# Moving the first parts of stationary weight blocks to the placement of their second parts

## The chip, the cores and the metric

The kernel runs on one core of one Trainium2 chip. The metric is device time in microseconds (us) of the whole kernel, which is one launch. An engine is named as in the profile: PE is the matrix engine, PEld its weight loads, DVE the vector engine, ACT the scalar engine, POOL the GpSimd engine, SP the engine that issues most DMAs.

## The reference, cut to what matters

The program is a two-layer decoder trunk on 256 positions of width 2048: a Mamba-2 layer and then a sparse-attention layer, each with a wide input projection, a gate and an output projection. Everything is fp32. The weights, some 230 MB, are read from HBM once. The change is about the two wide projections that are computed transposed, channels by positions:

```python
def ssd_mixer(x, w_in, conv_w, ...):
    proj = x @ w_in                      # 256 x 2048 by 2048 x 10304
    z, xbc, dt = jnp.split(proj, ...)
    ...
def dsa_mixer(x, w_in, ...):
    proj = x @ w_in
    c_q, c_kv, k_idx, w_idx, gate = jnp.split(proj, [s1, s2, s3, s4], -1)
    ...
    return (o * jax.nn.silu(gate)) @ w_out
```

## The kernel before, in words

**Products in parts.** PE multiplies in a format that is narrower than fp32 (`F32R`). To keep the precision, each fp32 operand is split into a first part `h` (its rounding to that format) and a second part `l` (what the rounding left). A product is then three matmuls: first by first, first by second, second by first. `Stream` does this for weights. A unit is one block of 128 x 1024 weights: SP loads it into one of four `raw` buffers (line 93), ACT rounds it into `h` (line 109), DVE subtracts to get `l` (line 138), and PE uses both. Four units are split ahead of the one that PE is on (`SPLIT`), so a unit's conversions are due some four units before its matmuls.

**The stage that the change touches.** `stream_w` (from line 306) computes 128 channels by 256 positions out of two units. The first unit of a pair (`half == 0`, use `FIRST8`) holds row tiles 0 to 7 of the 2048 input rows, the second (`half == 1`, use `OTHERS`) row tiles 8 to 15. A row tile is 128 x 128 weights, which PE holds stationary, while 256 columns of the input stream past them ("moving"). The input is stored as `xT` (in the second layer `x1T`): for each row tile 256 first parts, and right behind them 256 second parts. So each `h` tile is loaded twice in a row, once for each part of the input (line 328), and each `l` tile once (line 324). Each unit has 16 matmuls with `h` and 8 with `l`. In a `FIRST8` unit the `h` matmuls come first, in the order 0 to 7, and the `l` matmuls follow in the order 0, 1, 6, 7, 4, 5, 2, 3. In an `OTHERS` unit the `l` matmuls come first. There are 80 pairs of units in the first layer (accumulator `acc` in the trace) and 32 pairs in the second (`g`, the gate), which makes 112 pairs and 3584 matmuls with `h`. Between units the kernel puts the small matmuls of the scan and of the heads.

All other units have use `MOVING` or are read by other code: there the weights are cut in the same way, and none of their matmuls is touched.

**Where the parts lie.** `places` (line 123) gives each unit its two places in SBUF. The first part has a plain block of 1024 numbers (4096 bytes in each partition). The second part has a buffer of 1088 numbers (4352 bytes), and lies in it in one of three ways: for `FIRST8` as four chunks of 256 numbers that begin 272 numbers (1088 bytes) apart, for `OTHERS` as one block that begins 16 numbers (64 bytes) into the buffer, else as one block from its start. In the built program `xT` (byte 20,992), `x1T` (86,528) and all buffers of `h` (135,680 on, 4096 apart) and `l` (152,064 on, 4352 apart) begin at multiples of 256 bytes. A moving slice is 1024 bytes long and also begins at such a multiple; a row tile's weights are 512 bytes. What is called **offset** below is the start of the stationary weights less the start of the moving slice, in bytes, modulo 256:

| matmuls | offset before, by row tile |
|---|---|
| `h`, both kinds of unit | 0 for all |
| `l` of `FIRST8` | 0 for tiles 0 and 1, 64 for 2 and 3, 128 for 4 and 5, 192 for 6 and 7 |
| `l` of `OTHERS` | 64 for all |

**What sets the order.** The kernel is written under a manual schedule: each engine runs its instructions in the order in which the program issues them, and waits on semaphores where it reads what another engine writes. `Stream.run` issues a unit's conversions, its matmuls, and then one step of every piece of side work that is active. For a head of the attention layer one such step writes `og` (line 978, DVE), a later one rounds it (line 985, ACT), and the next subtracts (line 987, DVE); `og` has three buffers.

Of the kernel before, what the change touches and what calls it, by code (L numbers as in the profile page):

```python
# [9 lines left out]
F32 = mybir.dt.float32  # L10
F32R = mybir.dt.float32r
I32 = mybir.dt.int32
AF = mybir.ActivationFunctionType
# [3 lines left out]
P = 128  # L17
T = 256
# [41 lines left out]
MOVING, FIRST8, OTHERS = range(3)  # L60
# [9 lines left out]
class Stream:  # L70
# [22 lines left out]
            self.nc.sync.dma_start(r[:, :u.width], u.src)  # L93
            self.raws[i] = r

    def pieces(self, i):

        w = self.units[i].width
        n = w // 2 if i == 0 else w
        return [slice(a, a + n) for a in range(0, w, n)]  # L100

    def convert(self, i, eng, later=False):

        if i < len(self.units):
            w = self.units[i].width
            r = self.raws.pop(i)
            h, l = self.places(i)
            for cs in self.pieces(i):
                self.nc.scalar.activation(h[:, cs], r[:, cs], AF.Copy)  # L109
            self.parts[i] = (h, l)  # L110
            a, b = r[:, :w], h[:, :w].bitcast(F32)
            if len(l.shape) == 3:
                a, b = (t.rearrange("p (a b) -> p a b", a=4) for t in (a, b))
            else:
                l = l[:, :w]
            self.halfway[i] = (l, a, b)
        if not later:
            self.finish(i, eng)

    def places(self, i):  # L120

        if i in self.homes:
            pool, o = self.homes[i]
            return [pool.tile([P, 1088], F32R, tag=t, name=f"{t}{i}")[:, o:o + 1024]
                    for t in ("hi", "lo")]
        h = self.whi.tile([P, 1024], F32R, tag="hi", name=f"hi{i}")
        t = self.wlo.tile([P, 1088], F32R, tag="lo", name=f"lo{i}")  # L130
        use = self.units[i].use
        if use == FIRST8:
            return h, t.rearrange("p (a b) -> p a b", a=4)[:, :, 0:256]
        return h, t[:, 16:1040] if use == OTHERS else t[:, 0:1024]

    def finish(self, i, eng):
        if i in self.halfway:
# [33 lines left out]
def trunk_kernel(ctx: ExitStack, tc: tile.TileContext, x, xt, w1, wdt, dtp, prm, wo1,  # L171
                 wkv, wcq, wix, wg, wab, wo2, lnr, out):
    nc = tc.nc
# [15 lines left out]
    def acc_tile(name):  # L189
        return p_acc.tile([P, 512], F32, tag="acc", name=name)  # L190

    def y_tile(name):
        return p_y.tile([P, 512], F32, tag="y", name=name)
# [116 lines left out]
    def stream_w(half, cell, name, turn=True):  # L310


        def pe(h, l):
            if half == 0:
                cell["ps"] = acc_tile(name)[:, 0:T]
            ps, xs = cell["ps"], cell["x"][0]
            first, second = (1, 0) if half and turn else (0, 1)
            for lo in (first, second):
                for k in (0, 1, 6, 7, 4, 5, 2, 3) if lo and half == 0 else range(8):
                    kt, w = half * 8 + k, slice(k * P, (k + 1) * P)  # L320
                    last = half == 1 and lo == second and k == 7
                    if lo:
                        lw = l[:, w] if half else l[:, k // 2, k % 2 * P:(k % 2 + 1) * P]
                        nc.tensor.matmul(ps, lw, xs[:, kt, 0:T], start=False,  # L324
                                         stop=last, skip_group_check=True)
                    else:
                        for c in range(2):
                            nc.tensor.matmul(ps, h[:, w], xs[:, kt, c * T:(c + 1) * T],  # L328
                                             start=(kt == 0 and c == 0), stop=last and c == 1,
                                             skip_group_check=True)  # L330
        return pe
# [183 lines left out]
    for g in range(NG):  # L515
        for kind, n in (("B", 1), ("C", 1), ("x", 4), ("z", 4)):
            for ci in range(n):
                cell = {"x": xcell}
                for half in range(2):
                    k = len(st.units)  # L520
                    i = st.add(w1[k], 1024, stream_w(half, cell, f"acc{k}", turn=k > 1),
                               OTHERS if half else FIRST8)
# [72 lines left out]
    for g in range(NG):  # L595
        u = 20 * g
# [75 lines left out]
    for n in range(2):  # L672
        cs = slice(n * 1024, (n + 1) * 1024)
# [120 lines left out]
    for kb in range(8):  # L794
        i = st.add(wcq[kb], 1024, stream_tok(kb, 512, cells["q"], "qp",
                                             held if kb < EARLY else None), MOVING)
    st.side(i, (lat_norm, cells["q"], 512, PC_QG, 4, "q", "cqT"))
    for kb in range(8):
        i = st.add(wkv[kb], 672, stream_tok(kb, 336, cells["kv"], "kvp"), MOVING)
# [7 lines left out]
    def idx_pe(q, cell):  # L807
        def pe(h, l):
            cell["ps"] = acc_tile(f"ix{q}")
            for k in range(2):  # L810
                ps = cell["ps"][:, k * T:(k + 1) * T]
                for kt in range(4):
                    o = (k * 4 + kt) * P
                    nc.tensor.matmul(ps, h[:, o:o + P], cqT[:, kt, 0:T], start=(kt == 0), stop=False)
                    nc.tensor.matmul(ps, h[:, o:o + P], cqT[:, kt, T:2 * T], start=False, stop=False)
                    nc.tensor.matmul(ps, l[:, o:o + P], cqT[:, kt, 0:T], start=False, stop=(kt == 3))
        return pe
# [41 lines left out]
    for q in range(4):  # L859
        cell = {}  # L860
        i = st.add(wix[q], 1024, idx_pe(q, cell), MOVING)
# [68 lines left out]
    def head_steps(h):  # L930
        p, k = divmod(h, 2)
        (qh, ql, q1), (kh, kl, k1) = ([a[:, k, :] for a in PR[p][nm]] for nm in "qk")
        vh, vl, v2 = (a[:, k * P:(k + 1) * P] for a in PR[p]["v"])
        pl = y_tile(f"lg{h}")
        nc.tensor.matmul(pl[:, 0:128], q1, k1, start=True, stop=True)
        nc.tensor.matmul(pl[:, 128:384], qh, kh, start=True, stop=False)
        nc.tensor.matmul(pl[:, 128:384], qh, kl, start=False, stop=False)
        nc.tensor.matmul(pl[:, 128:384], ql, kh, start=False, stop=True)
        yield
        lg = d2.tile([P, 384], F32, tag="lg", name=f"lgs{h}")  # L940
        mx = d2.tile([P, 2], F32, tag="mx", name=f"mx{h}")
        sm = d2.tile([P, 2], F32, tag="sm", name=f"sm{h}")
        rn = d2.tile([P, 2], F32, tag="rn", name=f"rn{h}")
        parts = ((0, 0, 128), (1, 128, 384))
        for j, a, b in parts:
            v.tensor_tensor_reduce(out=lg[:, a:b], in0=pl[:, a:b], in1=mb[:, a:b],
                                   scale=-ATT_SCALE, scalar=3.0e38, op0=ALU.add, op1=ALU.min,
                                   accum_out=mx[:, j:j + 1])
        yield
        for j, a, b in parts:  # L950
            nc.scalar.activation(lg[:, a:b], lg[:, a:b], AF.Exp, scale=-1.0,
                                 bias=mx[:, j:j + 1], accum_out=sm[:, j:j + 1])
        yield
        v.reciprocal(rn, sm)
        for j, a, b in parts:
            v.tensor_scalar(lg[:, a:b], lg[:, a:b], rn[:, j:j + 1], 0.5,
                            op0=ALU.mult, op1=ALU.mult)
        yield
        yield
        pt = m_tile(f"pt{h}")  # L960
        for a in (0, 128, 256):
            nc.tensor.transpose(pt[:, a:a + 128], lg[:, a:a + 128], ident)  # L962
        yield
        ph, pl = (d2.tile([P, T], F32R, tag=f"prT{j}", name=f"prT{h}_{j}") for j in range(2))
        p2 = d2.tile([P, P], F32, tag="prT2", name=f"prT{h}_2")
        nc.scalar.activation(ph, pt[:, 0:T], AF.Copy)
        nc.scalar.activation(p2, pt[:, T:384], AF.Copy)
        v.tensor_sub(pl, pt[:, 0:T], ph.bitcast(F32))
        yield
        yield  # L970
        po = y_tile(f"o{h}")
        nc.tensor.matmul(po[:, 0:T], vh, ph, start=True, stop=False)
        nc.tensor.matmul(po[:, 0:T], vh, pl, start=False, stop=False)
        nc.tensor.matmul(po[:, 0:T], vl, ph, start=False, stop=False)
        nc.tensor.matmul(po[:, P:T], v2, p2, start=False, stop=True)
        yield
        og = d2.tile([P, T], F32, tag="og", name=f"og{h}", bufs=3)
        v.tensor_mul(og, po[:, 0:T], GT.pop(h))
        if h == 0:
            OG.append(big.tile([P, KT, 2 * T], F32R, tag="A", name="og0"))  # L980
        if h == 16:
            OG.append(big.tile([P, KT, 2 * T], F32R, tag="C", name="og1"))
        dst = OG[h // 16][:, h % 16, :]
        yield
        nc.scalar.activation(dst[:, 0:T], og, AF.Copy)
        yield
        v.tensor_sub(dst[:, T:2 * T], og, dst[:, 0:T].bitcast(F32))
        yield
# [3 lines left out]
    for p in range(NH2 // 2):  # L992
        src = wab[2 * p]
        i = st.add(wab[2 * p], 1024, pair_a(p), MOVING)
        st.side(i, (evac_steps, p, ("k", "v")))
        i = st.add(wab[2 * p + 1], 1024, pair_b(p), MOVING)
# [3 lines left out]
        n = (left * (p + 1)) // 16 - (left * p) // 16  # L1000
# [147 lines left out]
    d2 = L["d2"] = heads.enter_context(tc.tile_pool(name="d2", bufs=2))  # L1148
# [197 lines left out]
```

## Time and profile before

| | |
|---|---|
| median of 3 runs | 1253.55 us (1252.4 to 1253.58) |
| the profiled execution's own time | 1253.51 us |
| its span in the trace | 1251.6 us |
| PE busy | 1244.5 us, 99% of the span |
| PEld busy | 1162.4 us, 93% |
| DVE busy | 900.7 us, 72% |
| ACT busy | 667.4 us, 53% |
| PE clock granted | full speed all along |

The span is the time from the first instruction to the last, and lies 1.9 us below the execution's time. A matmul's duration in the trace includes the depth of the pipeline, so durations of successive matmuls overlap. How fast PE really goes is read from the chain of waits: where PE is the bound, a piece of that chain such as "3.84 ... x32" says that 32 matmuls followed each other in 3.84 us, which is 120 ns from one start to the next. This is called the **pitch** below.

### The profile page before, as it was taken

How to read it: one execution, taken by the hardware profiler on the slowest of the kernel's cores; microseconds unless marked ns; L12 is line 12 of the kernel's file. 1: busy time of each engine (PE TensorE's matmuls, PEld its weight loads, DVE VectorE, ACT ScalarE, POOL GpSimd, SP SyncE). 2: the span in 40 equal slices, each digit the busy share in tenths (PEclk: the TensorE clock that was granted, in tenths of full speed). 3: DMA queues.
4: the chain of work that ended last, by engine and by line, in shares of the span. 5: the costliest groups of instructions: out<-in, count | busy, mean ns of one | idle time of the engine just before them, and what ended most of it. 6: DMA issues, size and time to landing. Idle time of an engine off the chain costs nothing.

```text
span 1251.6 us, 22869 instructions
## 1 busy us (share of the span) xinstructions
PE 1244.5 (99%) x8981; PEld 1162.4 (93%) x8981; DVE 900.7 (72%) x1644; ACT 667.4 (53%) x1163; POOL 65.2 (5%) x102
## 2 busy tenths in 40 slices
PE   9999999999999999999999999999999999999998
PEld 8999999999999999888888899999999999888886
DVE  6868687888788878747556767867767777667457
ACT  5555555555555556534335655556666666434341
POOL 0001011001100110110000000000000000000000
PEclk9999999999999999999999999999999999999999
DMA  8655566566566665567666564555445455875662
GB/s 290 223 176 195 178 192 189 174 196 194 178 186 199 192 190 177 180 187 271 198 191 203 180 226 137 184 161 160 148 145 165 152 160 161 326 228 186 201 187 99
DMA packets 65372, 236.77 MB, mean 189 GB/s; under 512 B 8025, under 2 KB 8161, under 8 KB 64881
## 3 DMA queue, kind: packets, MB, share of 16 engines
q1 hardware_dynamic: 60352, 215.29, 54.1%
q0 software_dynamic: 4912, 20.02, 5.0%
q8 instruction: 71, 1.16, 0.4%
q14 instruction: 37, 0.30, 0.1%
HBM read 231.00 MB, written 4.28 MB: 188 GB/s over the span
## 4 chain that ended last, share of the span: by engine, by line
PE 99%; DMA 1%; SPq 0%; DVE 0%; ACT 0%; DVEq 0%; issue 0%
PE acc L328 25%; PE acc L324 12%; PE g L328 10%; PE o L546 9%; PE o L548 9%; PE o L547 9%; PE g L324 5%; PE y L443 2%; PE q L901 1%; PE q L900 1%; PE q L899 1%; PE pt L962 1%; PE pxs L423 1%; PE k L877 1%; PE k L879 1%; PE v L887 1%
## 5 line engine op out<-in xcount | busy, mean ns | idle before, releaser
L138 DVE TENSOR_TENSOR lo<-raw,hi 128x1024 fp32r<-128x1024 f32 (+1 forms) x404 | 489.9, 1215 | 288.1 <-ACT hi L109 286.4
L109 ACT ACTIVATE hi<-raw 128x1024 fp32r<-128x1024 f32 (+2 forms) x405 | 423.0, 1048 | 225.6 <-PE o L548 159.9
L328 PE MATMUL acc<-xT,hi 128*128 128x256 f32 x2560 | 328.3, 284 | 0.2 <-ACT hi L109 0.2
L328 PEld LDWEIGHTS acc<-xT,hi 128*128 128x128 f32 x2560 | 314.8, 192 | 2.3 <-ACT E L398 1.2
L324 PE MATMUL acc<-xT,lo 128*128 128x256 f32 x1280 | 165.4, 281 | 0.0
L324 PEld LDWEIGHTS acc<-xT,lo 128*128 128x128 f32 x1280 | 156.8, 189 | 0.0
L328 PE MATMUL g<-x1T,hi 128*128 128x256 f32 x1024 | 132.3, 284 | 0.0
L328 PEld LDWEIGHTS g<-x1T,hi 128*128 128x128 f32 x1024 | 126.0, 191 | 0.2
L546 PE MATMUL o<-hi,yg 128*128 128x512 f32 x256 | 100.3, 392 | 0.0
L547 PE MATMUL o<-lo,yg 128*128 128x512 f32 x256 | 99.6, 389 | 0.0
L548 PE MATMUL o<-hi,yg 128*128 128x512 f32 x256 | 99.6, 389 | 0.0
L546 PE MATMUL o<-hi,og 128*128 128x512 f32 (+1 forms) x256 | 99.5, 389 | 0.0
L548 PE MATMUL o<-hi,og 128*128 128x512 f32 (+1 forms) x256 | 98.9, 386 | 0.0
L547 PE MATMUL o<-lo,og 128*128 128x512 f32 (+1 forms) x256 | 98.8, 386 | 0.0
L347 DVE SCALAR_TENSOR_TENSOR ca<-acc,par,ca 128x255 f32<-128x255 f32 x144 | 69.0, 479 | 3.4
L324 PE MATMUL g<-x1T,lo 128*128 128x256 f32 x512 | 69.9, 281 | 0.0
L324 PEld LDWEIGHTS g<-x1T,lo 128*128 128x128 f32 x512 | 63.8, 189 | 0.2
L546 PEld LDWEIGHTS o<-hi,yg 128*128 128x128 f32 x256 | 48.1, 188 | 10.1 <-issue 0.2
L548 PEld LDWEIGHTS o<-hi,yg 128*128 128x128 f32 x256 | 48.1, 188 | 10.0
L547 PEld LDWEIGHTS o<-lo,yg 128*128 128x128 f32 x256 | 48.1, 188 | 9.9
L548 PEld LDWEIGHTS o<-hi,og 128*128 128x128 f32 x256 | 48.1, 188 | 9.9
L547 PEld LDWEIGHTS o<-lo,og 128*128 128x128 f32 x256 | 48.1, 188 | 9.6
(268 smaller groups left out, 1658.0 us busy)
## 6 DMA issues: line engine op xcount, KB each, us to landing
raw<-in_w_dram SPq DMA_DIRECT2D x160, 512.0 KB, 3.7
raw<-in_wo_dram SPq DMA_DIRECT2D x128, 512.0 KB, 4.1
raw<-in_wg_dram SPq DMA_DIRECT2D x64, 512.0 KB, 3.5
raw<-in_wab_dram SPq DMA_DIRECT2D x32, 512.0 KB, 3.7
abc<-acs_d POOLq DMA_DIRECT2D x32, 256.0 KB, 4.3
raw<-in_wcq_dram SPq DMA_DIRECT2D x8, 512.0 KB, 4.5
raw<-in_wkv_dram SPq DMA_DIRECT2D x8, 336.0 KB, 3.0
scr<-in_xt_dram SPq DMA_DIRECT2D x4, 512.0 KB, 7.1
```

What stands on the lines that cost most here:

```text
L109: self.nc.scalar.activation(h[:, cs], r[:, cs], AF.Copy)
L138: eng.tensor_sub(*self.halfway.pop(i))
L324: nc.tensor.matmul(ps, lw, xs[:, kt, 0:T], start=False, stop=last, skip_group_check=True)
L328: nc.tensor.matmul(ps, h[:, w], xs[:, kt, c * T:(c + 1) * T], start=(kt == 0 and c == 0), stop=last and c == 1, skip_group_check=True)
L347: v.scalar_tensor_tensor(acc[:, d:], ps[:, :T - d], w(k), acc[:, d:], op0=ALU.mult, op1=ALU.add)
L423: nc.tensor.transpose(pm[:, o:o + P], G[g][("x", 2 * half + c)][:, s * P:(s + 1) * P], ident)
L443: nc.tensor.matmul(py[ks, c * T + s * P:(c + 1) * T], xsT[:, s, c, ks], ms[c][k][:, ws], start=(c == 0 and s == 0), stop=(s == 1), skip_gr ...
L546: nc.tensor.matmul(ps, ah, hs, start=(kk == 2 * first), stop=False)
L547: nc.tensor.matmul(ps, ah, ls, start=False, stop=False)
L548: nc.tensor.matmul(ps, al, hs, start=False, stop=(kk == 31))
L877: nc.tensor.matmul(ps, h[:, o:o + P], ckvT[:, ct, 0:T], start=(ct == 0), stop=False)
L879: nc.tensor.matmul(ps, l[:, o:o + P], ckvT[:, ct, 0:T], start=False, stop=(ct == 1))
```

## The change

The first parts get the same places as the second parts. Both pools now hand out buffers of 1088 numbers, and both parts of a `FIRST8` unit lie in four chunks of 256 that are 272 apart, both parts of an `OTHERS` unit begin 16 numbers into their buffer. ACT writes the four chunks with one instruction whose output has two steps (128 x 4 x 256), DVE reads them back in the same form, and PE takes an `h` tile from its chunk. The very first unit is still rounded in two halves, now of two chunks each. To make room for the four wider buffers (4 x 256 bytes more in each partition), `og` has two buffers in place of three. What lies behind the first parts in SBUF moves up by 1024 bytes, which is a multiple of 256. The offsets of the `h` matmuls become those of the `l` matmuls: 0 for tiles 0 and 1 of a `FIRST8` unit, 64 for 2 and 3, 128 for 4 and 5, 192 for 6 and 7, and 64 for all of an `OTHERS` unit. No other matmul's offset changes. The order of the matmuls stays: `h` tiles go 0 to 7.

```diff
     def convert(self, i, eng, later=False):
 
         if i < len(self.units):
-            w = self.units[i].width
+            u = self.units[i]
             r = self.raws.pop(i)
             h, l = self.places(i)
-            for cs in self.pieces(i):
-                self.nc.scalar.activation(h[:, cs], r[:, cs], AF.Copy)
+            if u.use == FIRST8:
+                a = r.rearrange("p (a b) -> p a b", a=4)
+                n = 4 if i else 2
+                for c in range(0, 4, n):
+                    self.nc.scalar.activation(h[:, c:c + n], a[:, c:c + n], AF.Copy)
+                self.halfway[i] = l, a, h.bitcast(F32)
+            else:
+                w = u.width
+                self.nc.scalar.activation(h[:, :w], r[:, :w], AF.Copy)
+                self.halfway[i] = l[:, :w], r[:, :w], h[:, :w].bitcast(F32)
             self.parts[i] = (h, l)
...
     def places(self, i):
...
-        h = self.whi.tile([P, 1024], F32R, tag="hi", name=f"hi{i}")
-        t = self.wlo.tile([P, 1088], F32R, tag="lo", name=f"lo{i}")
         use = self.units[i].use
+        t = [pool.tile([P, 1088], F32R, tag=k, name=f"{k}{i}")
+             for pool, k in ((self.whi, "hi"), (self.wlo, "lo"))]
         if use == FIRST8:
-            return h, t.rearrange("p (a b) -> p a b", a=4)[:, :, 0:256]
-        return h, t[:, 16:1040] if use == OTHERS else t[:, 0:1024]
+            return [a.rearrange("p (a b) -> p a b", a=4)[:, :, 0:256] for a in t]
+        return [a[:, 16:1040] if use == OTHERS else a[:, 0:1024] for a in t]
...
                 for k in (0, 1, 6, 7, 4, 5, 2, 3) if lo and half == 0 else range(8):
-                    kt, w = half * 8 + k, slice(k * P, (k + 1) * P)
+                    kt = half * 8 + k
                     last = half == 1 and lo == second and k == 7
+                    wt = l if lo else h
+                    wt = (wt[:, k * P:(k + 1) * P] if half else
+                          wt[:, k // 2, k % 2 * P:(k % 2 + 1) * P])
...
-        og = d2.tile([P, T], F32, tag="og", name=f"og{h}", bufs=3)
+        og = d2.tile([P, T], F32, tag="og", name=f"og{h}")
```

No instruction changes its place on any engine. What changes is the form of ACT's roundings of `FIRST8` units. ACT, in the first layer, before (`hi` is the first part, `raw` the loaded block, the other rows are steps of the convolution):

```order
L109 ACTIVATE hi_385<-raw_241 128x1024
L354 ACTIVATE C_418<-ca_345 128x256
L343 ACTIVATE ca_420<-acc_353,par 128x256
L109 ACTIVATE hi_422<-raw_273 128x1024
L109 ACTIVATE hi_458<-raw_314 128x1024
```

and now:

```order
L106 ACTIVATE hi_385<-raw_241 128x4x256
L349 ACTIVATE C_418<-ca_345 128x256
L338 ACTIVATE ca_420<-acc_353,par 128x256
L110 ACTIVATE hi_422<-raw_273 128x1024
L106 ACTIVATE hi_458<-raw_314 128x4x256
```

The same roundings stand at the same places; those of `FIRST8` units are written in four chunks. On DVE, in the attention layer, these rows follow each other before (`og_9802`, `og_9907` and `og_10006` are the outputs of three successive heads, `og_9804` the array that collects them):

```order
L987 TENSOR_TENSOR og_9804<-og_9802,og_9804 128x256
L978 TENSOR_TENSOR og_9907<-o_9846,sC 128x256
L946 ISA lgs_9913,mx_9914<-lg_9858,mb 128x128
L946 ISA mx_9914 128x1
L946 ISA lgs_9913,mx_9914<-lg_9858,mb 128x256
L946 ISA mx_9914 128x1
L925 TENSOR_TENSOR hq_1_9920<-q_9881,hq_0_9919 128x256
L138 TENSOR_TENSOR lo_9926<-raw_9732,hi_9925 128x1024
L968 TENSOR_TENSOR prT_1_9963<-pt_9909,prT_0_9962 128x256
L138 TENSOR_TENSOR lo_9976<-raw_9776,hi_9975 128x1024
L987 TENSOR_TENSOR og_9804<-og_9907,og_9804 128x256
L978 TENSOR_TENSOR og_10006<-o_9957,sC 128x256
```

and now:

```order
L982 TENSOR_TENSOR og_9804<-og_9802,og_9804 128x256
L973 TENSOR_TENSOR og_9907<-o_9846,sC 128x256
L941 ISA lgs_9913,mx_9914<-lg_9858,mb 128x128
L941 ISA mx_9914 128x1
L941 ISA lgs_9913,mx_9914<-lg_9858,mb 128x256
L941 ISA mx_9914 128x1
L920 TENSOR_TENSOR hq_1_9920<-q_9881,hq_0_9919 128x256
L131 TENSOR_TENSOR lo_9926<-raw_9732,hi_9925 128x1024
L963 TENSOR_TENSOR prT_1_9963<-pt_9909,prT_0_9962 128x256
L131 TENSOR_TENSOR lo_9976<-raw_9776,hi_9975 128x1024
L982 TENSOR_TENSOR og_9804<-og_9907,og_9804 128x256
L973 TENSOR_TENSOR og_10006<-o_9957,sC 128x256
```

Nothing moved; with two buffers `og_10006` takes the place of `og_9802`, whose last reader stands eleven rows ahead of it on the same engine.

More of the change, by code (lines that the diff above doesn't have):

```diff
@@ L94, in load @@
             self.raws[i] = r
-    def pieces(self, i):
-        w = self.units[i].width
-        n = w // 2 if i == 0 else w
-        return [slice(a, a + n) for a in range(0, w, n)]
     def convert(self, i, eng, later=False):
         if i < len(self.units):
-            w = self.units[i].width
+            u = self.units[i]
             r = self.raws.pop(i)
             h, l = self.places(i)
-            for cs in self.pieces(i):
-                self.nc.scalar.activation(h[:, cs], r[:, cs], AF.Copy)
-            self.parts[i] = (h, l)
[L111 to L116, printed above, removed]
+            if u.use == FIRST8:
[8 more added lines that the diff above has]
+                self.halfway[i] = l[:, :w], r[:, :w], h[:, :w].bitcast(F32)
+            self.parts[i] = (h, l)
         if not later:
@@ L319, in pe @@
                 for k in (0, 1, 6, 7, 4, 5, 2, 3) if lo and half == 0 else range(8):
-                    kt, w = half * 8 + k, slice(k * P, (k + 1) * P)
+                    kt = half * 8 + k
                     last = half == 1 and lo == second and k == 7
+                    wt = l if lo else h
+                    wt = (wt[:, k * P:(k + 1) * P] if half else
+                          wt[:, k // 2, k % 2 * P:(k % 2 + 1) * P])
                     if lo:
-                        lw = l[:, w] if half else l[:, k // 2, k % 2 * P:(k % 2 + 1) * P]
-                        nc.tensor.matmul(ps, lw, xs[:, kt, 0:T], start=False,
+                        nc.tensor.matmul(ps, wt, xs[:, kt, 0:T], start=False,
                                          stop=last, skip_group_check=True)
@@ L327, in pe @@
                         for c in range(2):
-                            nc.tensor.matmul(ps, h[:, w], xs[:, kt, c * T:(c + 1) * T],
+                            nc.tensor.matmul(ps, wt, xs[:, kt, c * T:(c + 1) * T],
                                              start=(kt == 0 and c == 0), stop=last and c == 1,
```

## The prediction

> **What bounds the kernel now.** I read the page first: engines, granted clock, chain.
>
> ```profile
> span 1251.6 us, 22869 instructions
> PE 1244.5 (99%) x8981; PEld 1162.4 (93%) x8981; DVE 900.7 (72%) x1644; ACT 667.4 (53%) x1163; POOL 65.2 (5%) x102
> PEclk9999999999999999999999999999999999999999
> PE 99%; DMA 1%; SPq 0%; DVE 0%; ACT 0%; DVEq 0%; issue 0%
> PE acc L328 25%; PE acc L324 12%; PE g L328 10%; PE o L546 9%; PE o L548 9%; PE o L547 9%; PE g L324 5%; PE y L443 2%; PE q L901 1%; PE q L900 1%; PE q L899 1%; PE pt L962 1%; PE pxs L423 1%; PE k L877 1%; PE k L879 1%; PE v L887 1%
> ```
>
> PE works without a pause at full clock, and the chain that ended last is PE alone. A change that touches neither the number nor the order of matmuls can only tell through their pitch. The `h` matmuls of line 328 are 35% of the chain, so I asked next how fast they go. The groups:
>
> ```profile
> L328 PE MATMUL acc<-xT,hi 128*128 128x256 f32 x2560 | 328.3, 284 | 0.2 <-ACT hi L109 0.2
> L324 PE MATMUL acc<-xT,lo 128*128 128x256 f32 x1280 | 165.4, 281 | 0.0
> L328 PE MATMUL g<-x1T,hi 128*128 128x256 f32 x1024 | 132.3, 284 | 0.0
> ```
>
> The shapes are the same, yet one with `h` lasts 284 ns and one with `l` 281. Pipelined durations don't add up, so the pitch has to come from the chain in order of time. In the first layer (start, us, what):
>
> ```profile
> 367.45 1.88 PE acc L324 x16
> 369.33 3.84 PE acc L328 x32
> ...
> 368.39 0.94 PE acc L324 x8
> ```
>
> Thirty-two `h` matmuls take 3.84 us, 120.0 ns each. The 16 `l` matmuls ahead of them take 1.88 us, 117.5 ns each, and the last row is the `OTHERS` half of those alone (offset 64): 0.94 us for 8, the same 117.5. Narrow windows cut the `FIRST8` half into its pairs, offsets 0, 192, 128 and 64 in this order:
>
> ```profile
> 367.45 0.24 PE acc L324 x2
> ...
> 367.69 0.23 PE acc L324 x2
> ...
> 367.92 0.23 PE acc L324 x2
> ...
> 368.15 0.24 PE acc L324 x2
> ```
>
> At 0.01 us for two, these only say that no offset is worse than 120 and that the middle two run at some 115. In the second layer there is a faster pitch still, between heads:
>
> ```profile
> 846.33 0.12 PE lg L936
> 846.45 0.12 PE lg L937
> 846.57 0.12 PE lg L938
> 846.68 0.91 PE g L324 x8
> 847.59 3.84 PE g L328 x32
> 851.43 0.94 PE g L324 x8
> ```
>
> Here an `OTHERS` eight takes 0.91 us, 113.75 ns a matmul, at the same offset 64 that cost 117.5 above. What differs is what came just before: head matmuls at offset 0 (lines 936 to 938), not `l` matmuls at offset 64. So offset 64 has two pitches, and the history decides which. Of the 112 `OTHERS` eights, 16 are of the quick kind (0.91 or 0.92 us), all of them behind line 938.
>
> Two things could make `h` slower than `l` other than its place: each `h` tile is loaded twice in a row, and `h` meets both halves of the input. The query projection has both traits with weights of the same shape (lines 899 and 900 load one tile twice), at another offset (224):
>
> ```profile
> 1010.95 0.12 PE q L899
> ...
> 1013.64 0.12 PE q L901
> 1013.75 0.33 PE pt L962 x3
> ```
>
> Its 24 matmuls run from 1010.95 to 1013.75, 116.7 ns each. The key projection is alike at offset 192:
>
> ```profile
> 1006.95 0.13 PE k L877
> ...
> 1008.26 0.12 PE k L879
> 1008.37 0.12 PE v L886
> ```
>
> Twelve in 1.42 us, 118.3 ns. Double loading does not cost 120; the place is what is left.
>
> The Trainium skill says otherwise: the page "SBUF — State Buffer", section "Who interferes with whom", has PE waiting for no one in SBUF, and "TensorE: Matmul & The Clock Gate", "Step-by-step: what each phase is for", gives it two independent read ports, one for moving and one for stationary data. By these, no placement could change a pitch, and the sum below would be zero. The trace disagrees: 113.75 against 117.5 and 120 ns for one shape.
>
> **The change, part by part.** *Offsets.* Of 3584 `h` matmuls, 448 (tiles 0 and 1 of 112 `FIRST8` units, twice each) stay at offset 0 and 120 ns. 1792 in `OTHERS` units go to 64; in `FIRST8` units 448 each go to 64, 128 and 192.
>
> `OTHERS`: the 16 `h` matmuls follow 8 `l` matmuls at the same offset, so I take the pitch to be handed on. In 96 units that is 117.5: 96 x 16 x 2.5 ns = 3.84 us. In the 16 quick ones it is 113.75: 16 x 16 x 6.25 = 1.60 us. Together 5.44.
>
> `FIRST8`, offset 64: these four come behind offset 0, as the quick eights did, but from the 120 pitch. Between 117.5 and 113.75 no row decides, so I take the middle, 115.6: 448 x 4.4 = 1.97 us. Offsets 128 and 192: the `l` pairs at about 115 have just stepped down by 64 bytes, while `h` steps up; line 877's 118.3 is a run at 192. I take 117.5: 896 x 2.5 = 2.24 us.
>
> The `l` matmuls keep their places; only the first pair of a `FIRST8` unit is now entered from 192 instead of 0. I leave this at nothing: a nanosecond either way is 0.1 us over 112 units.
>
> Sum: 5.44 + 1.97 + 2.24 = 9.65 us. From the profiled execution's own 1253.51 us (span 1251.6 and 1.9 around it; 0.04 below the median) this leaves 1243.9.
>
> Bounds: with only the steady rows, 1792 + 448 at 117.5 and nothing from 128 and 192, the gain is 2240 x 2.5 = 5.6 us; if each of four changes of offset in a `FIRST8` unit also costs the 10 ns by which the first matmul of the key run exceeds its others (0.13 against 0.12), 4 x 112 x 10 = 4.5 goes off, and 1.1 is left. At the other end all 3136 run at 113.75: 19.6 us. The sum stands near the middle, since over half of it, the 5.44, goes by pitches that the same offset shows now.
>
> *ACT writes four chunks, DVE reads them.* The nearest rows are the input's own rounding, which already writes 1024 numbers as four chunks of 256, and DVE's subtractions, of which those for `FIRST8` already write that form:
>
> ```profile
> L614 ACT ACTIVATE xT<-scr 128x1024 fp32r<-128x1024 f32 x2 | 2.1, 1062 | 0.5 <-DMA scr<-in_xt_dram 0.4
> L109 ACT ACTIVATE hi<-raw 128x1024 fp32r<-128x1024 f32 x1 | 1.1, 1061 | 0.2 <-DMA raw<-in_w_dram 0.2
> L138 DVE TENSOR_TENSOR lo<-raw,hi x404: 850/1225/1228, 10.6 to 1226.6; 128x1024 fp32r<-128x1024 f32 x133, 128x672 fp32r<-128x672 f32 x2
> ```
>
> 1062 against 1061 ns, and no subtraction above 1228 (minimum, median, maximum): chunks cost nothing that shows. Were it otherwise, there is cover, as stretches of both stages show (PE, PEld, DVE, ACT, POOL):
>
> ```profile
> 100.00:200.00 100.00, 100.00 (x845) 98.00 (x844) 74.83 (x122) 55.55 (x90) 9.94 (x13) 1.00 0.59 185
> 800.00:900.00 100.00, 100.00 (x854) 100.00 (x854) 72.04 (x172) 61.26 (x146) 0.00 (x0) 1.00 0.53 160
> ```
>
> DVE is idle for 25 us in 100. A pair takes at least 48 pitches of some 119 ns, 5.7 us, so at most 17 pairs fall in 100 us, and a chunked subtraction could take 1.4 us longer before DVE ran behind PE; without that cover every further 0.1 us would cost 11 us over 112 pairs. DMA share is 0.59: a PE that is 1% faster asks for 1% more.
>
> *og with two buffers.* A write now needs the head before last to be done with its buffer. That reader is DVE's own subtraction, ahead in DVE's queue, so no engine is held up by the missing buffer: nothing. The cover is DVE's order; were it gone, ACT's rounding (line 985), which that subtraction already waits for, would be the one to wait for.
>
> **The rivals.** (1) *The quick pitch spreads.* At offset 64 a quick matmul hands quickness on, and `FIRST8` units step from 0 to 64 each time. If 128 and 192 are quick as well and `OTHERS` units inherit it, all 3136 run at 113.75: 1253.5 − 19.6 = 1233.9. For it: the 0.91 row. Against: the `FIRST8` eight of `l` ends slow now whatever its middle pairs do, and the `OTHERS` `h` come behind `OTHERS` `l`, so their 96 units have no reason to change.
>
> (2) *No change:* the 120 ns belongs to line 328's way of alternating two moving halves that lie end to end (the second begins where the first stops), which lines 899 and 877 share only in part, as three matmuls a tile break the alternation. Then 1253.5. It is also where the skill's ports lead. Against: the pitch of 0.24 for the `l` pair at offset 0, the same 120 as `h`.
>
> (3) *Slower: offsets 128 and 192 clash when stepped up to.* In `h` each lasts for four matmuls, in `l` for two, and no row holds 128 for longer. The rest gains 5.44 + 1.97 = 7.4 us; the 896 matmuls at 128 and 192 eat that at 7.4 / 896 = 8.3 ns over today's 120, so the change is slower from 128.3 on. At the 130 of the key run's first row the loss is 9.0 and the time 1253.5 + 1.6 = 1255.1. For it: that row. Against: the other eleven of that run, at the same offset 192, are at 0.12.
>
> **How the numbers follow.** The forecast has 0.70, with a range of its own from 1239.7 to 1247.9 (gains of 13.8, where all 1344 `FIRST8` matmuls beyond tile 1 run at 113.75 and 5.44 + 8.4 is saved, and of 5.6). Rival 1 has 0.14, rival 2 has 0.10, rival 3 has 0.06. A range of 1236.5 to 1250.5 holds the forecast, most of what lies between it and rival 1's end, and the smaller gains near the low bound. This kernel's measurement can tell 0.2%, 2.5 us, from no change. Faster is the forecast and rival 1, 0.84; same is rival 2, 0.10; slower is rival 3, 0.06.
>
> **What would show it.** In the chain, an `OTHERS` unit's 16 `h` matmuls at 1.88 us, 1.82 behind heads, in place of 1.92; a `FIRST8` unit's 16 at about 1.88, its first four still at 0.48. Line 328's mean falls from 284 to about 281; lines 109 and 138, and the pitch of the output projections and of `l`, stay. PE's share stays at 99%. I am wrong if line 328 keeps 3.84 for 32, if PE begins to wait for ACT or DVE, or if the gain sits in other lines.

## The result

The changed kernel takes 1234.03 us (median of 4 runs, 1233.92 to 1234.32) against 1253.49 of the kernel before in the same comparison. The ratio is 0.9847, with a 95% interval from 0.983 to 0.9864: 19.5 us less. The forecast was 1243.9, so the direction was right and the size half of what came. The time lies below the range, and on the number of the first rival (1233.9).

The page of the changed kernel, engines and chain:

```profile
span 1232.1 us, 22869 instructions
PE 1225.6 (99%) x8981; PEld 1143.6 (93%) x8981; DVE 900.1 (73%) x1644; ACT 667.1 (54%) x1163; POOL 65.0 (5%) x102
PE 99%; DMA 1%; SPq 0%; DVE 0%; ACT 0%; DVEq 0%; issue 0%
```

Nothing but PE has changed: 18.9 us less busy with the same number of instructions, still 99% of the span, and still the whole chain. DVE and ACT are as busy as before to 0.6 us. The groups of both projections, and the conversions:

```profile
L131 DVE TENSOR_TENSOR lo<-raw,hi 128x1024 fp32r<-128x1024 f32 (+1 forms) x404 | 489.7, 1215 | 274.1 <-ACT hi L110 256.9 <-ACT hi L106 16.1
L323 PE MATMUL acc<-xT,hi 128*128 128x256 f32 x2560 | 317.4, 280 | 0.2 <-ACT hi L106 0.2
L319 PE MATMUL acc<-xT,lo 128*128 128x256 f32 x1280 | 162.7, 279 | 0.0
L323 PE MATMUL g<-x1T,hi 128*128 128x256 f32 x1024 | 127.8, 279 | 0.0
L106 ACT ACTIVATE hi<-raw 128x1024 fp32r<-128x1024 f32 (+1 forms) x113 | 118.5, 1049 | 27.4 <-PE acc L323 21.6 <-PE g L323 2.9 <-DMA raw<-in_w_dram 1.8
```

The `h` matmuls (line 323 now) fell from 284 to 280 and 279 ns. The `l` matmuls of the first layer (line 319) fell too, from 281 to 279, though their places did not change. ACT's write of four chunks (line 106) takes 1049 ns in the mean, and DVE's mean stays at 1215: the chunks cost nothing. The chain in order of time, first layer:

```profile
364.67 3.71 PE acc L323 x32
368.37 0.94 PE acc L319 x8
369.31 0.44 PE pxs L418 x4
369.75 0.92 PE acc L319 x8
370.67 1.82 PE acc L323 x16
...
372.92 1.89 PE acc L323 x16
```

A piece of side work (`pxs`) happens to part the two units here. The `FIRST8` unit's 16 `h` matmuls (last row) take 1.89 us, 118 ns each, and its eight `l` 0.94. The `OTHERS` unit's eight `l` take 0.92 and its 16 `h` 1.82, 113.75 ns each: quick as a whole, where it had 0.94 and 1.92. In the second layer, behind heads, the same:

```profile
835.23 0.94 PE g L319 x8
...
837.20 0.12 PE lg L933
837.32 0.91 PE g L319 x8
838.23 1.81 PE g L323 x16
```

Summed over the starts of all successive matmuls of the two traces, the time went as follows:

| matmuls | predicted | measured |
|---|---|---|
| `h` of `FIRST8` (1792) | −4.2 us | −3.5 us |
| `h` of `OTHERS` (1792) | −5.4 us | −11.7 us |
| `l` of `FIRST8` (896) | 0 | +0.1 us |
| `l` of `OTHERS` (896) | 0 | −3.0 us |
| everything else on PE | 0 | −1.3 us |

The predicted 4.2 for `FIRST8` is the sum's 1.97 + 2.24. The last row is spread over small matmuls whose places did not change, none of them with more than 0.5 us.

### The profile page after: what moved, and what is told of

Read it like the earlier page. It is cut to its first block, busy times and chain, and to the rows that moved or that the text cites. A ratio compares the mean times of both kernels' runs of the same rounds, so it can differ in the third digit from the quotient of the medians.

```text
span 1232.1 us, 22869 instructions
## 1 busy us (share of the span) xinstructions
PE 1225.6 (99%) x8981; PEld 1143.6 (93%) x8981; DVE 900.1 (73%) x1644; ACT 667.1 (54%) x1163; POOL 65.0 (5%) x102
## 4 chain that ended last, share of the span: by engine, by line
PE 99%; DMA 1%; SPq 0%; DVE 0%; ACT 0%; DVEq 0%; issue 0%
PE acc L323 24%; PE acc L319 12%; PE g L323 10%; PE o L541 9%; PE o L543 9%; PE o L542 9%; PE g L319 5%; PE y L438 2%; PE q L895 1%; PE q L896 1%; PE q L894 1%; PE pt L957 1%; PE pxs L418 1%; PE k L873 1%; PE k L872 1%; PE k L874 1%
## 5 line engine op out<-in xcount | busy, mean ns | idle before, releaser
L131 DVE TENSOR_TENSOR lo<-raw,hi 128x1024 fp32r<-128x1024 f32 (+1 forms) x404 | 489.7, 1215 | 274.1 <-ACT hi L110 256.9
L110 ACT ACTIVATE hi<-raw 128x1024 fp32r<-128x1024 f32 (+1 forms) x292 | 305.1, 1048 | 191.1 <-PE o L543 155.8
L323 PE MATMUL acc<-xT,hi 128*128 128x256 f32 x2560 | 317.4, 280 | 0.2 <-ACT hi L106 0.2
L323 PEld LDWEIGHTS acc<-xT,hi 128*128 128x128 f32 x2560 | 304.0, 188 | 2.3 <-ACT E L393 1.2
L319 PE MATMUL acc<-xT,lo 128*128 128x256 f32 x1280 | 162.7, 279 | 0.0
L106 ACT ACTIVATE hi<-raw 128x1024 fp32r<-128x1024 f32 (+1 forms) x113 | 118.5, 1049 | 27.4 <-PE acc L323 21.6
L323 PE MATMUL g<-x1T,hi 128*128 128x256 f32 x1024 | 127.8, 279 | 0.0
L323 PEld LDWEIGHTS g<-x1T,hi 128*128 128x128 f32 x1024 | 121.7, 188 | 0.2
```

The source lines that it names most:

```text
L106: self.nc.scalar.activation(h[:, c:c + n], a[:, c:c + n], AF.Copy)
L110: self.nc.scalar.activation(h[:, :w], r[:, :w], AF.Copy)
L131: eng.tensor_sub(*self.halfway.pop(i))
L319: nc.tensor.matmul(ps, wt, xs[:, kt, 0:T], start=False, stop=last, skip_group_check=True)
L323: nc.tensor.matmul(ps, wt, xs[:, kt, c * T:(c + 1) * T], start=(kt == 0 and c == 0), stop=last and c == 1, skip_group_check=True)
```

## The experiments

All edits below are made to the changed kernel, but for the last one. Two theories stood against each other. **The entry decides**: at offset 64 there are two pitches, what ran just before decides which, and it is then kept. The four-chunk `FIRST8` unit, with both parts moved, now ends quick and hands that on. **Own placement**: a unit is quick as soon as all of its own weights lie at 64. Where eights are counted below, eight successive matmuls of one part are called quick where their mean pitch, from each start to the next, is under 115 ns, and slow from 115 to 119. Single gaps above 130 ns are left out of these means: a trace has 82 of them, most of some 200 ns.

**Only `FIRST8` first parts moved.**

```diff
-        return [a[:, 16:1040] if use == OTHERS else a[:, 0:1024] for a in t]
+        if use == OTHERS:
+            return t[0][:, 0:1024], t[1][:, 16:1040]
+        return [a[:, 0:1024] for a in t]
```

> Only the first parts of FIRST8 units move; those of OTHERS units stay at offset 0. Theory (the entry decides): the new places in the FIRST8 unit change the pitch with which its second parts end, so the OTHERS second parts behind them stay quick (0.91 us for 8, in place of 0.94), while the OTHERS first parts are back at 120 ns (1.92 us for 16). The table of the changed kernel gives 3.5 us for the FIRST8 first parts and 3.0 us for the OTHERS second parts, so about 1247. Rival (an OTHERS unit is quick because all of its own weights lie at 64): the OTHERS second parts go back to 0.94, and only the 3.5 us are left: 1250.

Measured: 1246.38 us, ratio to before 0.9948 [0.9932, 0.9965]. In its chain:

```profile
376.00 0.92 PE acc L321 x8
376.92 1.92 PE acc L325 x16
...
379.27 1.86 PE acc L325 x16
```

The `OTHERS` second parts are quick (0.92) though nothing in their unit was touched, and the first parts at offset 0 behind them are at 120 ns. The entry decides; own placement would have left 0.94 and 1250. In this run and in the changed kernel, the second parts of `OTHERS` are quick in all 78 pairs in which nothing stands between the two units; in the kernel before they are slow in all 78.

**Only `OTHERS` first parts moved.**

```diff
         if use == FIRST8:
-            return [a.rearrange("p (a b) -> p a b", a=4)[:, :, 0:256] for a in t]
+            a, b = (a.rearrange("p (a b) -> p a b", a=4)
+                    for a in (t[0][:, 0:1024], t[1]))
+            return a, b[:, :, 0:256]
```

> Only the first parts of OTHERS units move to 64; FIRST8 units are as in the kernel before. Theory (the entry decides): the FIRST8 second parts end as they did before and hand on the slow pitch, so the OTHERS first parts run at 117.5 ns (1.88 us for 16) but behind heads at 113.75: a gain of 5.4 us, 1248. Rival (own placement): the OTHERS unit is quick as a whole, 24 matmuls at 113.4: 1792 x 6.6 = 11.8 us for the first parts and 3.0 us for the second, 1239.

Measured: 1246.76 us, ratio 0.9952 [0.9937, 0.9967].

```profile
377.85 0.94 PE acc L321 x8
378.80 1.89 PE acc L325 x16
```

With all weights of the `OTHERS` unit at 64, it runs slow here, as it was entered: 0.94 and 1.89. (Behind heads it is quick, as its second parts were before.) This is the pitch that the prediction had taken for the whole change; its 5.4 us for these matmuls came out as 5.5, by the starts of successive matmuls. Own placement, which gave 1239, falls. The two halves of the change bring 6.4 and 6.0 us against their common comparison (1252.73); together they bring 19.5. Most of the 7 us between are the `OTHERS` first parts turned from slow to quick (11.7 in place of 5.5), which takes both halves.

**The second parts of `FIRST8` in plain order.** They then end at offset 192, not 64.

```diff
-                for k in (0, 1, 6, 7, 4, 5, 2, 3) if lo and half == 0 else range(8):
+                for k in range(8):
```

> The changed kernel with the FIRST8 second parts in the order 0 to 7, so that they end at offset 192 instead of 64. Theory (the entry decides): the pitch handed to the OTHERS unit is another one, and as a step from 192 to 64 was slow in the kernel before (121 ns and then 117 to 118), its 24 matmuls go back to about 117.5: 112 x 24 x 4.1 ns = 11 us more than the changed kernel, 1245. Rival (own placement): the OTHERS unit stays at 113.4, and the time at 1234 within 1.5.

Measured: 1238.68 us, ratio 0.9887 [0.9873, 0.9902]: some 5 us above the changed kernel, between the two expectations. The chain in the first layer and behind heads in the second:

```profile
382.02 1.87 PE acc L319 x16
383.90 1.81 PE acc L323 x16
```

```profile
867.04 0.12 PE lg L933
867.16 0.94 PE g L319 x8
```

and the changed kernel at this last pair:

```profile
864.35 0.91 PE g L319 x8
```

In the first layer the `OTHERS` unit is quick by its first parts (1.81 for 16). In the second its eight takes 0.94, where the changed kernel has 0.91 behind the same head. The same placement gives either pitch, and the end of the unit before decides, even through the head's matmuls. The guess that a step from 192 to 64 always leads to the slow pitch was wrong; the kernel before, which it named, has no such step, as its `l` tiles there go 0, 192, 128, 64.

**All units at 64, no chunks.**

```diff
-            return [a.rearrange("p (a b) -> p a b", a=4)[:, :, 0:256] for a in t]
+            return [a[:, 16:1040].rearrange("p (a b) -> p a b", a=4) for a in t]
```

> Both parts of both kinds of unit lie as one block at offset 64; there are no steps of the offset inside a pair. Theory (the entry decides, and a pitch at one offset is kept until something else comes between): a pair runs wholly quick (48 x 113.4 = 5.44 us, 0.10 us less than the changed kernel's 5.55 by the trace) or wholly slow (48 x 117.5 = 5.64). All quick would be 1222, all slow 1245; what side work leaves behind decides, and I expect a mixture nearer to slow, about 1240. Rival (own placement at 64 is quick of itself): 1222.

Measured: 1232.71 us, ratio 0.984 [0.9825, 0.9854], not told apart from the changed kernel. Of its 672 eights 367 are quick and 305 slow. In the first layer whole stretches between two pieces of side work are of one kind, at the latest from their second eight on. A slow one:

```profile
233.54 0.22 PE pxs L418 x2
233.75 1.89 PE acc L323 x16
235.64 1.89 PE acc L319 x16
237.53 3.77 PE acc L323 x32
241.29 1.88 PE acc L319 x16
```

Every row of `acc` is at 117.5 to 118 ns, 80 matmuls in a row, with nothing to turn it. The mixture was expected, but nearer to slow. What side work does to the pitch depends on what ran ahead of it as well as on the kind of work. The 16 matmuls of `y`, where they alone stand between two units, turn it over, here from slow to quick:

```profile
139.65 1.88 PE acc L323 x16
141.54 1.45 PE y L438 x16
...
145.02 1.81 PE acc L319 x16
```

Of the seven such places in this run six are of this kind. At the first, at 80 us, the stretch ahead is quick and the one behind is slow.

**`FIRST8` first parts as one block at 64, second parts in chunks.**

```diff
-            return [a.rearrange("p (a b) -> p a b", a=4)[:, :, 0:256] for a in t]
+            a, b = (a.rearrange("p (a b) -> p a b", a=4)
+                    for a in (t[0][:, 16:1040], t[1]))
+            return a, b[:, :, 0:256]
```

> As the changed kernel, but the FIRST8 first parts lie as one block at 64, and only the FIRST8 second parts are in four chunks. Theory (the entry decides): if the sequence 0, 192, 128, 64 of the second parts still ends quick, the OTHERS unit and the next FIRST8 first parts are quick, 40 matmuls at 113.4 and 8 at about 118, 5.48 us a pair against 5.55 in the changed kernel: 112 x 0.07 = 8 us less, and some of it lost where side work comes between, so about 1228. If the sequence, now entered from 64, ends slow, the other 40 run at 117.5: 5.64 a pair, 1244. Rival (own placement at 64 is quick of itself): 1226 whatever the entry, which the block at 64 in all parts has already spoken against.

Measured: 1240.03 us, ratio 0.9896 [0.9879, 0.9912]. 522 of 672 eights are slow:

```profile
363.69 3.77 PE acc L325 x32
367.46 1.88 PE acc L321 x16
```

So the chunks of the second parts end slow here as they did in the kernel before. This holds even where the first parts ahead of them ran quick. It is the chunked first parts ahead of them, which end at 192, that make them end quick; no run tells whether their last offset does it or their whole sequence. The time lies below the 1244 expected of "slow", since 150 eights are quick after all.

**One block at other offsets**, for both parts of both kinds of unit (one run each, but for 64). The edit is the one of "all units at 64" with the block's start at 0, 32, 48, 12, 20 or 24 numbers in place of 16, for `FIRST8` and `OTHERS` alike:

```diff
-            return [a.rearrange("p (a b) -> p a b", a=4)[:, :, 0:256] for a in t]
-        return [a[:, 16:1040] if use == OTHERS else a[:, 0:1024] for a in t]
+            return [a[:, 32:1056].rearrange("p (a b) -> p a b", a=4) for a in t]
+        return [a[:, 32:1056] if use == OTHERS else a[:, 0:1024] for a in t]
```

> Both parts of both kinds of unit at offset 0. Theory (the offset sets the possible pitches): every matmul of the two projections goes at 120 ns, 3.84 us for 32; against the kernel before the second parts lose what they had, 1792 x 2.5 ns and a little more for the 16 quick eights, 5 us: 1258. Rival (a pitch of 120 comes from line 323 alternating two halves that lie end to end): the second parts stay near 117.5 and the time near 1253.

> Both parts of both kinds of unit at offset 128, with no steps in a pair. The prediction took 117.5 ns for this offset: 48 x 117.5 = 5.64 us a pair, 1245. A quick pitch as at 64 would give 1222 to 1233, a clash above 120 more than 1258.

> Both parts of both kinds of unit at offset 192, with no steps in a pair. The prediction took 117.5 ns for this offset too, and the key projection's run at it has 118.3: about 1245 to 1247. A quick pitch as at 64 would give 1222 to 1233.

> Both parts of both kinds of unit as one block at offset 48, 16 bytes before the offset that has a quick and a slow pitch. If what counts is the 64-byte piece that a block begins in, 48 lies in the same piece as 0 and gives 120 ns and 1257. If the pitch goes smoothly with the distance, it lies between 0 and 64: 116 to 118 ns, 1238 to 1246. If only the quick pitch is left here, 113.4 throughout and 1222.

> Both parts of both kinds of unit as one block at offset 80, 16 bytes past 64. If the 64-byte piece counts, as at 64: a mixture of 113.4 and 117.5, about 1233. If the distance counts smoothly, between 64 and 128: 116 to 119, 1238 to 1250. If only the quick pitch is left here, 1222.

> Both parts of both kinds of unit as one block at offset 96, half way from 64 to 128 (1233 and 1251). If the 64-byte piece counts, as at 64: about 1233. If the distance counts smoothly, about 1242. If only the quick pitch is left here, 1222.

Measured:

| offset | 0 | 48 | 64 | 80 | 96 | 128 | 192 |
|---|---|---|---|---|---|---|---|
| us | 1257.29 | 1256.98 | 1232.71 | 1251.37 | 1247.18 | 1251.17 | 1243.73 |

From the chains at 0, 128 and 192:

```profile
118.00 1.92 PE acc L319 x16
119.92 3.84 PE acc L323 x32
```

```profile
117.36 1.90 PE acc L319 x16
119.25 3.80 PE acc L323 x32
```

```profile
73.09 3.63 PE acc L323 x32
76.72 1.81 PE acc L319 x16
...
120.49 1.89 PE acc L319 x16
```

and at 48:

```profile
118.91 1.97 PE acc L319 x16
...
137.32 1.89 PE acc L319 x16
```

At offset 0 the second parts go at 120 ns like the first, 1.92 for 16. They neither alternate between two halves nor load a tile twice, so the second rival's reason for the 120 falls with the run. At 128 the pitch is 119 ns, where the prediction took 117.5. At 192 it is mostly 118, but 63 of the 672 eights are quick, at the same 113.4 as at 64. From 41 to 80 us 42 of them follow each other, with eight matmuls of `pxs` between, and the 16 of `y` end them. So 192 has the same two lasting pitches as 64, and was merely seldom entered quick. 16 bytes before or behind 64, at 48 and 80, the quick pitch is gone. At 48 there are two others: 438 eights run at 118 ns and 234 at 123, by the starts and without the gaps above 190 ns. So 48 takes the time of 0, where most run at 120, by a mixture of two other pitches. At 80, 96 and 128 the eights lie between 117 and 121 ns, with no clear split. So the times at 48, 64 and 192 are those of mixtures and not of the offset alone. Neither "the 64-byte piece" (80 is far from 64, 96 too) nor a smooth course (80 is slower than 96) fits all seven. As the input was never moved, these runs don't tell the distance between the two blocks from the place of the weights alone.

**Four chunks only where side work ends.** This takes the unit that is held to be the cause and puts it into a kernel that otherwise lies at 64 throughout. In `RESET` are 50 of the 112 `FIRST8` units: the 49 that stand right behind side work, and the second of all. Side work inside a pair is not followed by chunks.

```diff
...
+        self.pair = -1
...
         if use == FIRST8:
-            return [a.rearrange("p (a b) -> p a b", a=4)[:, :, 0:256] for a in t]
+            self.pair += 1
+            if self.pair in RESET:
+                return [a.rearrange("p (a b) -> p a b", a=4)[:, :, 0:256] for a in t]
+            return [a[:, 16:1040].rearrange("p (a b) -> p a b", a=4) for a in t]
```

> All units at offset 64, but the first FIRST8 unit after each piece of side work (50 of the 112) lies in four chunks, as in the changed kernel. Theory (a four-chunk unit turns the pitch quick, and it stays quick at 64 until side work comes between): all units behind a four-chunk one are quick, at 0.91 us for 8, up to the next side work; the 50 units themselves cost 2.83 us against 2.72. From 1232.7 with 305 of 672 eights slow to about 1228.5. Rival (the pitch goes with something else that side work leaves behind): the same eights stay slow behind the four chunks, and the 50 units come on top: 1233 to 1236.

Measured: 1227.26 us, ratio 0.9795 [0.9779, 0.9811]. The stretch that was slow above:

```profile
233.50 1.85 PE acc L326 x16
235.35 3.63 PE acc L330 x32
238.98 1.81 PE acc L326 x16
240.79 3.63 PE acc L330 x32
244.42 0.91 PE acc L326 x8
```

From the `OTHERS` unit on every row is at 113.1 to 113.75 ns: 3.63 for 32, where there was 3.77. The units behind the four-chunk one have the same place in both kernels. Of the eights 511 are quick now, in place of 367. The four-chunk unit is the cause, and its effect lasts at least until side work comes between. This version is faster than both kernels: its ratio's interval lies below that of the changed kernel, 0.983 to 0.9864.

With the chunks only in the 19 `FIRST8` units right behind side work whose stretch was slow:

> The same, with four chunks only in the 19 FIRST8 units whose entry after side work was slow in the run with all units at 64. Theory: if the other entries stay quick, 1225; as a changed pitch before side work may change the one after it, some entries may turn slow: up to 1231. Rival: 1233 to 1235.

Measured: 1229.38 us, ratio 0.9812 [0.9798, 0.9827], 472 quick eights. Six entries that had been quick without chunks turned slow once the stretch before them was quick, as the expectation allowed. All six stand behind the 16 matmuls of `y`, which turn the pitch over. It is no better than the version with more chunks.

**Two `og` buffers in the kernel before.**

```diff
-        og = d2.tile([P, T], F32, tag="og", name=f"og{h}", bufs=3)
+        og = d2.tile([P, T], F32, tag="og", name=f"og{h}")
```

> The kernel before with two og buffers in place of three, and nothing else. The prediction costed this at nothing, since the buffer's last reader stands ahead of the next write on the same engine: 1253 within 1. Rival (a write of og waits, and heads run later): PE gains waits of up to 0.4 us for each of 32 heads, 1253 to 1266.

Measured: 1253.17 us beside 1253.31 of the kernel before (one run each). The missing buffer costs nothing.

## Why the prediction was half right

**What bounds the kernel: right.** PE alone set the end, no engine's wait took over what PE gave up, and the gain is pitch. Double loading and the alternating halves were rightly ruled out as causes of the 120 ns; the run at offset 0 shows it.

**`h` of `FIRST8`: right in size, partly by luck.** 4.2 us were predicted and 3.5 came. Offsets 128 and 192 brought 1.1 and 1.2 us, as the 2.24 for both had it, and offset 64 brought 0.9 of 1.97. The step from 0 to 64 was given 115.6 ns, between quick and slow, and the first layer's trace has 117.8 for tiles 2 and 3: from the 120 pitch it leads to the slow one, not to the quick one as behind the heads. Offset 128 alone is at 119, not 117.5, but as two tiles between steps it came out at 117.7. The tiles that stay at 0 gave 0.4 us that the sum did not have.

**`h` of `OTHERS`: the mechanism right, the entry wrong.** The prediction said that the pitch is handed on from the `l` matmuls to the `h` behind them, and "Only `OTHERS` first parts moved" shows just that. The step that failed is the one before it. The prediction left the `l` matmuls at nothing, saying of the first pair of a `FIRST8` unit, "now entered from 192 instead of 0", that "a nanosecond either way is 0.1 us over 112 units". Against the first rival it held that "the `FIRST8` eight of `l` ends slow now whatever its middle pairs do". The first treats only the eight's duration, which indeed stayed at 0.94 us, and the second takes for granted that it goes on ending as it did. What changed is the state in which the eight ends. Behind the chunked first parts, whose last tiles lie at 192, it ends quick; behind a block at 0 or at 64 it ends slow. That state reaches over 24 matmuls of the next unit: 11.7 in place of 5.4 us for `h`, and 3.0 us for `l` that had no line in the sum.

**The rivals.** The first rival's time, 1233.9, was met within 0.2 us, which is luck. Its `OTHERS` units did inherit a quick pitch. But it had all 3136 moved matmuls at 113.75, `FIRST8` too; these stayed at some 118, and the `OTHERS` second parts and smaller things made up the difference. Both arguments held against it took for granted that the `FIRST8` eight goes on ending slow, so its chance of 0.14 was too low.

**No change** fell, as `h` left 120 ns though line 323 alternates its halves as before. **Slower** fell too: blocks at 128 and 192 run at 119 and 118 ns, not at the 128.3 and more that it needed. By the section "Who interferes with whom" of the page "SBUF — State Buffer" in the Trainium skill, PE waits for no one. The runs disagree with what the prediction drew from this, that no placement could change a pitch: with the same instructions in the same order, seven placements of the weights gave 1232.7 to 1257.3 us.

**What stays open.** The runs show that offset and entry decide, and which sequences end quick. They don't show what in PE or in SBUF the two pitches are, why 64 and 192 have these two, 48 has two others and 80 has none, nor why one piece of side work turns the pitch and another leaves it.

## What to carry to other kernels

Where PE is the bound and each matmul loads new weights, measure the pitch from the chain for every placement of the stationary block against the moving one: here it ranged from 113.4 to 123 ns at equal shapes. Look for two pitches at one placement before costing a change with the one that a row shows, and ask what state each group leaves behind, not only how long it takes. A kernel's time at one placement can be that of a mixture, so count the states in its trace before ranking placements by time. A sequence that ended in the quick state in all 78 pairs without side work inside, put once behind each interruption of a kernel at 64, was worth more (25.6 us against before) than the same sequence in every pair (19.5).

## What was not expected of the hardware

At offsets 64 and 192 two pitches, 113.4 and 117.5 to 118 ns, each last for as long as the same kind of matmul follows: up to 27 eights in a row were slow in "all units at 64". What ran before can tell through other matmuls in between: behind the same head an eight takes 0.91 or 0.94 us, by how the unit before the head ended, while the 16 matmuls of `y` turn one pitch into the other. Moving all blocks by 16 bytes, from 64 to 80 or to 48, costs 19 and 24 us of 1233 (one run each).
